# Two groups of tiles change places in SBUF: the split sums of a seven-product scheme and the raw weight blocks it works on

## The chip, the core and the metric

The kernel runs on one core of a Trainium2 chip. The metric is the device time of one execution in microseconds (us). TensorE (PE) multiplies, VectorE (DVE) and ScalarE (ACT) do elementwise work, GpSimd (POOL) does a few small operations, and SyncE (SP) issues most of the DMA transfers. SBUF is the on-chip memory: 128 partitions, each a row of bytes. A tile has the same byte range in every partition.

## The reference, cut to what matters

Two decoder layers over 256 tokens of width 1024. Each layer is a half-step SwiGLU FFN, a token mixer, and a second half-step FFN, with a layer norm behind each.

```python
def swiglu(x, wg, wu, wd):
    return (jax.nn.silu(x @ wg) * (x @ wu)) @ wd
...
    for l in range(DEPTH):
        x = layer_norm(ALPHA * x + 0.5 * swiglu(x, ffn_wg[l, 0], ffn_wu[l, 0], ffn_wd[l, 0]), ln_g[l, 0], ln_b[l, 0])
        m = token_mix(x, w_in[l], w_out[l], cmp_pe[l], cmp_w1[l], cmp_w2[l], pool_w[l], pool_scale[l],
                      gla_wa2[l], gla_ba[l], gla_norm_g[l])
        x = layer_norm(ALPHA * x + m, ln_g[l, 1], ln_b[l, 1])
        x = layer_norm(ALPHA * x + 0.5 * swiglu(x, ffn_wg[l, 1], ffn_wu[l, 1], ffn_wd[l, 1]), ln_g[l, 2], ln_b[l, 2])
```

So there are four FFNs (called FFN 1 to 4 here) and two token mixers, one between FFN 1 and 2, one between FFN 3 and 4. The token mixer compresses keys and values (this uses `cmp_w1`, 1 MB in its expanded form), and computes attention scores.

## The kernel before

**Precision.** Every float32 operand of a large product is split in two parts (`hi` or `wh`: a rounded copy that ACT writes; `lo` or `wl`: the rest, that DVE subtracts). One product is three matmuls: hi by hi, hi by rest, rest by hi. The activations are the stationary operand (128 by 128), the weights the moving one (128 by 512).

**Weights.** A weight block of 512 KB (a tile of 128 by 1024) is loaded by SP into a `raw` tile (four of them rotate), split by ACT (L229) and DVE (L230) into `wh` and `wl` (eight of each rotate), and used by PE. Units of two blocks are made one to three units ahead of PE.

**The pairs.** In the middle part of each FFN six of the eleven gate/up chunks are done in three pairs S4, S6, S8 with seven products for eight: `seven` loads the raw blocks `fa` (b11), `fb` (b12), `fc` (b22) and a `raw` (b21) and subtracts them from one another in place; `make_sums` builds, once for each FFN, four split sums of the quarters of the activation stream, `sa0`, `sa1` and the two halves of `sb`. Products 1, 2 and 4 of a pair use quarters of the stream as they are (`xh`, `xl`), products 5, 6, 7 and 3 use the split sums. Each product is 12 matmuls of line L415. The order of all this is written out by hand and kept:

```python
PLAN = ("a2 T0 b2 S4 1 a3 5 b3 6 T2 d0 7 d1 3 4 2 S6 d2 1 5 T4 d3 6 a10 7 b10 3 4 2 "
        "S8 1 d4 5 T6 6 d5 T10 7 d6 3 4 2 d7 T8").split()
```

A number is a product, `d` a down projection (L262 to L264 on `hi`, `lo`), `T` the transposes of two finished chunks (L490) and their split into `hi` and `lo` (L267, L268), `a` and `b` ordinary gate/up chunks. After the plan come the down projections d10, d8, d9, a layer norm and the next stage.

**Places.** Tiles with the same tag of a pool share one place, and a new tile waits until the last use of the one before it there. A pool's tiles lie one behind another in the order in which the tags first occur. Tags that matter here:

| tag (pool) | bytes of a partition | tiles that take turns in it before |
|---|---|---|
| `ksh`, `ksl` (`cst`) | 25120, 29216 (4096 each) | `sa0`, `sa1`; the mixer's split keys (read by all attention scores) |
| `s_w1` (`cst`) | 16928 (8192) | `sb`; the mixer's compression weight `s_w1` |
| `qs0`, `qs1` (`mix`) | 180992, 185088 (4096 each) | `fa` (two blocks); the mixer's queries |
| `fb0`, `fb1` (`wp`) | 121600, 125696 (4096 each) | `fb` alone (two blocks) |

The pool `cst` also holds small constants; one of them, `mhalf`, takes 32 bytes, and so all tiles of `cst` behind it start 32 bytes past a multiple of 128. The tiles of `wp`, `act` (`xh`, `xl`) and of `mix` up to `pT` start at multiples of 128.

**The compression weight.** The mixer's small tensors are loaded by `layer_small` (L535). For layer 0 it is called at S8 of FFN 1 and its transfers go through SP's queue; for layer 1 they go through POOL's queue. The tile `s_w1` can be loaded when the tile ahead of it in its place has been read for the last time: `sb` is last read by product 3 of S8. `compress` reads `s_w1` in L665, in the mixer.

Of the kernel before, what the change touches and what calls it, by code (L numbers as in the profile page):

```python
# [18 lines left out]
F32 = mybir.dt.float32  # L19
F32R = mybir.dt.float32r  # L20
# [37 lines left out]
def build(ctx, tc, d):  # L58
# [3 lines left out]
    cst = ctx.enter_context(tc.tile_pool(name="cst", bufs=1))  # L62
    wp = ctx.enter_context(tc.tile_pool(name="wp", bufs=1))
    act = ctx.enter_context(tc.tile_pool(name="act", bufs=1))
    mix = ctx.enter_context(tc.tile_pool(name="mix", bufs=2))
# [52 lines left out]
    for t in range(2):  # L118
        vbd.append(cst.tile([128, 2, 2, 64], F32, name=f"vbd{t}"))
        a = cst.tile([128, 4, 128], F32, name=f"at{t}")  # L120
# [11 lines left out]
    def gate_up(l, f, c, q):  # L132
        return [d["wgu"][l, f, c, 2 * q + h] for h in range(2)]

    def seven(l, f, c):


        b11, b12, b21, b22 = [], [], [], []

        def load(to, src, pool, name, tags, bufs):  # L140
            for a, tag in zip(src, tags):
                to.append(pool.tile([128, 1024], F32, name=name, tag=tag, bufs=bufs))
                last_dma[0] = nc.sync.dma_start(out=to[-1], in_=a)

        def less(a, b, to):
            for x, y, z in zip(a, b, to):
                DVE.tensor_sub(out=z, in0=x, in1=y)  # L147

        def parts(ts):
            return [split_tile(x, 1024) for x in ts]  # L150

        def f1():
            load(b11, gate_up(l, f, c, 0), mix, "fa", ("qs0", "qs1"), 1)
            return parts(b11)

        def f5():
            load(b12, gate_up(l, f, c + 1, 0), wp, "fb", ("fb0", "fb1"), 1)
            less(b12, b11, b11)
            return parts(b11)

        def f6():
            load(b22, gate_up(l, f, c + 1, 1), mix, "fc", ("pT", "pT"), 3)
            less(b22, b11, b11)
            return parts(b11)

        def f7():
            less(b22, b12, b12)
            return parts(b12)

        def f4():  # L170
            load(b21, gate_up(l, f, c, 1), wp, "raw", ("raw", "raw"), 4)
            less(b21, b11, b11)
            return parts(b11)

        return {"1": f1, "5": f5, "6": f6, "7": f7, "3": lambda: parts(b22), "4": f4, "2": lambda: parts(b21)}

    for l in range(L):
# [37 lines left out]
    def split_tile(raw, w):  # L215
        wh, wl = split_tiles()
        ACT.activation(out=wh[:, :w], in_=raw[:, :w], func=AF.Copy)  # L217
        DVE.tensor_sub(out=wl[:, :w], in0=raw[:, :w], in1=wh[:, :w].bitcast(F32))  # L218
        return wh, wl
# [46 lines left out]
    def split(hi, lo, src):  # L266
        ACT.activation(out=hi, in_=src, func=AF.Copy)  # L267
        DVE.tensor_sub(out=lo, in0=src, in1=hi.bitcast(F32))  # L268
# [41 lines left out]
    def make_sums(sums):  # L310

        s1, a11, a12, a21 = sums["s"], sums[0, 0], sums[0, 1], sums[1, 0]
        big = cst.tile([128, 2, 2, 4, 128], F32R, name="sb", tag="s_w1")

        def parts(f, i):
            tl = cst.tile([128, 2, 4, 128], F32R, name=f"sa{i}", tag=("ksh", "ksl")[i]) if i < 2 else big[:, i - 2]
            split(tl[:, 0], tl[:, 1], f.rearrange("p (a b) -> p a b", a=4))
            return tl[:, 0], tl[:, 1]
        first = parts(s1, 0)
        DVE.tensor_sub(out=s1, in0=s1, in1=a11)  # L320
        DVE.tensor_sub(out=a21, in0=a11, in1=a21)
        DVE.tensor_sub(out=a12, in0=a12, in1=s1)
        yield first
        yield parts(s1, 1)
        yield parts(a21, 2)
        yield parts(a12, 3)
# [39 lines left out]
    class Ffn:  # L366
# [51 lines left out]
        def plan(self):  # L418
            a = [[tuple(p[:, 4 * q:4 * q + 4] for p in XT[t]) for q in range(2)] for t in range(2)]
            left = {"1": a[0][0], "2": a[0][1], "4": a[1][1]}  # L420
            sums = make_sums(self.sums)

            def f32():
# [691 lines left out]
```

## Time and profile before

| | |
|---|---|
| median of 3 runs | 977.65 us (976.71 to 978.5) |
| profiled execution, its own time | 978.65 us |
| its span, first to last instruction | 976.9 us |
| mean granted TensorE clock | 0.998 |
| PE busy | 960.0 us (98% of the span), 4611 matmuls |
| DVE busy | 843.0 us (86%) |
| ACT busy | 583.8 us (60%) |
| DMA moved | 178.80 MB, mean 183 GB/s |

The profile shows one execution. A matmul's record overlaps the next one's, so the pace of PE is read from the starts of its matmuls, or from the chain that ended last, where a piece lasts until the next begins. "Idle before" is the time in which an engine ran nothing, with what ended it. Times in a row are from the span's start.

### The profile page before, as it was taken

The numbers are of one execution on the slowest core, as the hardware profiler recorded it, in microseconds if no ns is written. First come the engines' busy times: TensorE is split into PE (matmuls) and PEld (weight loads), VectorE is DVE, ScalarE is ACT, GpSimd is POOL, SyncE is SP. The second block draws the span as 40 slices with busy tenths as digits, with TensorE's granted clock in tenths as the row PEclk, the third lists the DMA queues.
The fourth block names the chain that finished last, engine by engine and source line by source line (L and its number), as shares of the span: only waits on it lengthen the run. The fifth ranks groups of instructions, "written<-read, shape, count | busy, mean of one in ns | idle before, by whom it ended". The sixth has DMA issues, their size and how long they took to land.

```text
span 976.9 us, 12852 instructions
## 1 busy us (share of the span) xinstructions
PE 960.0 (98%) x4611; PEld 780.8 (80%) x4611; DVE 843.0 (86%) x1247; ACT 583.8 (60%) x884; POOL 34.7 (4%) x50
## 2 busy tenths in 40 slices
PE   8999999999999999999999999999999999999996
PEld 5888888778778888888788888878787788888885
DVE  6988997988869997999899799978887599899995
ACT  6666665566654666666565666655676366666660
POOL 0000000020001000000000000001000010000000
PEclk9999999999999999999999999999999999999999
DMA  8865666564444645638673746465534374647241
GB/s 282 320 200 169 208 213 237 185 193 144 139 163 141 210 156 189 206 138 280 200 241 119 241 129 225 138 247 186 178 109 137 123 222 148 212 151 237 93 167 43
DMA packets 51872, 178.80 MB, mean 183 GB/s; under 512 B 6624, under 2 KB 7648, under 8 KB 51552
## 3 DMA queue, kind: packets, MB, share of 16 engines
q1 hardware_dynamic: 49968, 171.23, 52.6%
q0 software_dynamic: 1840, 6.75, 2.3%
q8 instruction: 36, 0.59, 0.2%
q14 instruction: 28, 0.23, 0.1%
HBM read 176.91 MB, written 1.05 MB: 182 GB/s over the span
## 4 chain that ended last, share of the span: by engine, by line
PE 86%; DVE 6%; DMA 4%; ACT 2%; issue 2%; SPq 0%; DVEq 0%; ACTq 0%
PE g L415 12%; PE acc L264 11%; PE acc L262 11%; PE acc L263 11%; PE tr L415 8%; PE g L262 4%; PE g L263 4%; PE g L264 4%; PE tr L264 3%; PE tr L263 3%; PE tr L262 3%; DMA raw<-in_wd 3%; PE tr L290 3%; PE acc L281 2%; DVE wl L230 2%
## 5 line engine op out<-in xcount | busy, mean ns | idle before, releaser
L230 DVE TENSOR_TENSOR wl<-raw,wh 128x1024 fp32r<-128x1024 f32 (+2 forms) x225 | 266.7, 1201 | 42.3 <-ACT wh L229 40.9
L229 ACT ACTIVATE wh<-raw 128x1024 fp32r<-128x1024 f32 (+2 forms) x225 | 231.3, 1039 | 113.4 <-PE acc L264 55.4
L217 ACT ACTIVATE wh<-fa 128x1024 fp32r<-128x1024 f32 x96 | 101.7, 1060 | 87.3 <-DVE fa L147 44.3
L264 PE MATMUL acc<-wh,lo 128*128 128x512 f32 x352 | 137.7, 391 | 2.0 <-DVE lo L268 2.0
L262 PE MATMUL acc<-wh,hi 128*128 128x512 f32 x352 | 138.6, 394 | 0.0
L263 PE MATMUL acc<-wl,hi 128*128 128x512 f32 x352 | 137.1, 390 | 0.0
L218 DVE TENSOR_TENSOR wl<-fa,wh 128x1024 fp32r<-128x1024 f32 x96 | 116.4, 1220 | 17.9 <-ACT wh L217 16.3
L263 PE MATMUL g<-wl,xh 128*128 128x512 f32 (+1 forms) x224 | 85.6, 382 | 1.3 <-DVE wl L230 1.3
L264 PE MATMUL g<-wh,xl 128*128 128x512 f32 (+1 forms) x224 | 85.6, 382 | 0.0
L262 PE MATMUL g<-wh,xh 128*128 128x512 f32 (+1 forms) x224 | 85.2, 381 | 0.0
L264 PEld LDWEIGHTS acc<-wh,lo 128*128 128x128 f32 x352 | 66.1, 188 | 17.2 <-DVE lo L268 3.3
L262 PEld LDWEIGHTS acc<-wh,hi 128*128 128x128 f32 x352 | 66.1, 188 | 13.8 <-ACT hi L267 0.5
L263 PEld LDWEIGHTS acc<-wl,hi 128*128 128x128 f32 x352 | 66.1, 188 | 13.4
L263 PE MATMUL acc<-wl,xh 128*128 128x512 f32 x128 | 51.4, 402 | 1.0 <-DVE wl L230 1.0
L262 PE MATMUL acc<-wh,xh 128*128 128x512 f32 x128 | 51.0, 400 | 0.5 <-ACT wh L229 0.5
L264 PE MATMUL acc<-wh,xl 128*128 128x512 f32 x128 | 50.8, 397 | 0.0
L262 PE MATMUL tr<-wh,xh 128*128 128x512 f32 x128 | 50.2, 392 | 0.0
L264 PE MATMUL tr<-wh,xl 128*128 128x512 f32 x128 | 49.9, 390 | 0.0
L263 PE MATMUL tr<-wl,xh 128*128 128x512 f32 x128 | 49.8, 389 | 0.0
L263 PEld LDWEIGHTS g<-wl,xh 128*128 128x128 f32 x224 | 42.1, 188 | 9.5 <-DVE wl L230 2.1
L262 PEld LDWEIGHTS g<-wh,xh 128*128 128x128 f32 x224 | 42.2, 188 | 8.1 <-issue 0.8
L264 PEld LDWEIGHTS g<-wh,xl 128*128 128x128 f32 x224 | 42.1, 188 | 7.1
(287 smaller groups left out, 1937.1 us busy)
## 6 DMA issues: line engine op xcount, KB each, us to landing
raw<-in_wgu SPq DMA_DIRECT2D x103, 512.0 KB, 4.2
raw<-in_wd SPq DMA_DIRECT2D x88, 512.0 KB, 4.5
raw<-in_win SPq DMA_DIRECT2D x32, 512.0 KB, 4.3
fa<-in_wgu SPq DMA_DIRECT2D x24, 512.0 KB, 4.1
fb<-in_wgu SPq DMA_DIRECT2D x24, 512.0 KB, 4.5
fc<-in_wgu SPq DMA_DIRECT2D x24, 512.0 KB, 4.7
raw<-in_wout SPq DMA_DIRECT2D x16, 512.0 KB, 3.9
lnp_ln_g<-in_ln_g POOLq DMA_DIRECT2D x5, 512.0 KB, 5.2
```

The source lines that it names most:

```text
L217: ACT.activation(out=wh[:, :w], in_=raw[:, :w], func=AF.Copy)
L218: DVE.tensor_sub(out=wl[:, :w], in0=raw[:, :w], in1=wh[:, :w].bitcast(F32))
L229: ACT.activation(out=wh[:, s], in_=raw[:, s], func=AF.Copy)
L230: DVE.tensor_sub(out=wl[:, s], in0=raw[:, s], in1=wh[:, s].bitcast(F32))
L262: pe(PE.matmul(ps, xh, wh, start=start, stop=False))
L263: pe(PE.matmul(ps, xh, wl, start=False, stop=False))
L264: pe(PE.matmul(ps, xl, wh, start=False, stop=stop))
L281: PE.matmul(out, lhsT, rhs, start=False, stop=True, skip_group_check=True)
L290: last_pe[0] = PE.transpose(p[:, i * 128:(i + 1) * 128], s, ident)
L415: pe(PE.matmul(ps, a[:, k, :], w[:, s], start=first and k == 0 and n == 0, stop=k == 3 and n == 2, skip_group_check=True))
```

## The change

The sums go where the raw blocks were, and the raw blocks where the sums were: `sa0`, `sa1` take `qs0`, `qs1` of the pool `mix`; `sb` takes a place of 8192 bytes in `wp` (tag `fb`); `fa` takes `ksh`, `ksl`; and `fb`, now one tile of two blocks, takes `s_w1`. No engine instruction and no transfer is added or removed; sizes are the same.

```diff
         def load(to, src, pool, name, tags, bufs):
-            for a, tag in zip(src, tags):
-                to.append(pool.tile([128, 1024], F32, name=name, tag=tag, bufs=bufs))
+            whole = cst.tile([128, 2, 1024], F32, name=name, tag=tags) if pool is cst and len(tags[0]) == 1 else None
+            for i, (a, tag) in enumerate(zip(src, tags)):
+                to.append(whole[:, i] if whole is not None else pool.tile([128, 1024], F32, name=name, tag=tag, bufs=bufs))
                 last_dma[0] = nc.sync.dma_start(out=to[-1], in_=a)
...
         def f1():
-            load(b11, gate_up(l, f, c, 0), mix, "fa", ("qs0", "qs1"), 1)
+            load(b11, gate_up(l, f, c, 0), cst, "fa", ("ksh", "ksl"), 1)
             return parts(b11)
 
         def f5():
-            load(b12, gate_up(l, f, c + 1, 0), wp, "fb", ("fb0", "fb1"), 1)
+            load(b12, gate_up(l, f, c + 1, 0), cst, "fb", "s_w1", 1)
             less(b12, b11, b11)
             return parts(b11)
...
-        big = cst.tile([128, 2, 2, 4, 128], F32R, name="sb", tag="s_w1")
+        big = wp.tile([128, 2, 2, 4, 128], F32R, name="sb", tag="fb", bufs=1)
 
         def parts(f, i):
-            tl = cst.tile([128, 2, 4, 128], F32R, name=f"sa{i}", tag=("ksh", "ksl")[i]) if i < 2 else big[:, i - 2]
+            tl = (mix.tile([128, 2, 4, 128], F32R, name=f"sa{i}", tag=("qs0", "qs1")[i], bufs=1) if i < 2
+                  else big[:, i - 2])
             split(tl[:, 0], tl[:, 1], f.rearrange("p (a b) -> p a b", a=4))
```

## Rows read from the trace of the kernel before

**Rows 1.** The page, part 1: busy us, share of the span, instructions.
```profile
PE 960.0 (98%) x4611; PEld 780.8 (80%) x4611; DVE 843.0 (86%) x1247; ACT 583.8 (60%) x884; POOL 34.7 (4%) x50
```
**Rows 2.** Waits of PE: who, for whom; us in total, times, longest.
```profile
PE acc L264 <- DVE lo L268: 2.0, 3, 0.8
```
**Rows 3.** Timeline of PE, ends of FFN 1, 2, 3: start, us, what, idle before.
```profile
176.54 0.50 PE L264 MATMUL acc<-wh,lo 128*128 128x512 f32 x1 [0.65 <-DVE lo L268]
...
475.91 0.50 PE L264 MATMUL acc<-wh,lo 128*128 128x512 f32 x1 [0.50 <-DVE lo L268]
...
657.17 0.51 PE L264 MATMUL acc<-wh,lo 128*128 128x512 f32 x1 [0.84 <-DVE lo L268]
```
**Rows 4.** Chain that ended last, 120 to 180 us: start, us, what.
```profile
121.05 8.24 PE tr L415 x36
129.29 2.72 PE g L415 x12
...
137.46 2.79 PE g L415 x12
...
150.06 0.76 DVE lo L268 x2
...
158.73 4.62 DMA raw<-in_wd
...
165.80 7.66 DMA raw<-in_wd
...
175.80 0.69 DVE lo L268
```
**Rows 5.** Instructions of L415: ns min/median/max, first and last start, forms.
```profile
L415 PE MATMUL g<-wh,sa x128: 392/395/478, 53.2 to 923.6; 128*128 128x512 f32 x128
...
L415 PE MATMUL g<-wh,sb x128: 392/395/476, 70.6 to 940.6; 128*128 128x512 f32 x128
...
L415 PE MATMUL g<-wh,xh x96: 389/389/393, 45.0 to 945.5; 128*128 128x512 f32 x96
```
**Rows 6.** Instructions on the tiles hi: columns as in rows 5.
```profile
L262 PE MATMUL acc<-wh,hi x352: 387/389/501, 65.0 to 968.2; 128*128 128x512 f32 x176
```
**Rows 7.** Timeline of SP: start, us, DMA issues.
```profile
144.10 1.43 SPq L143 DMA_DIRECT2D fb<-in_wgu  x2
...
160.89 0.33 SPq L535 DMA_DIRECT2D s_w<-in_w  x1
161.31 4.82 SPq L226 DMA_DIRECT2D raw<-in_wd  x4
```
**Rows 8.** Chain that ended last, whole span: ends of FFN 2 and 3.
```profile
467.63 5.20 DMA raw<-in_wgu
...
645.99 6.73 DMA raw<-in_wd
```
**Rows 9.** Waits of POOL: columns as in rows 2.
```profile
POOL s_w L535 <- PE g L415: 141.2, 1, 141.2
```
**Rows 10.** Timeline of DVE, 142 to 146 us.
```profile
142.82 2.35 DVE L218 TENSOR_TENSOR wl<-fb,wh 128x1024 fp32r<-128x1024 f32 x2
```
**Rows 11.** Instructions on the tile s_w, 220 to 240 us: columns as in rows 5.
```profile
L665 PE MATMUL tr<-zB,s_w x16: 275/275/275, 228.4 to 230.1; 128*128 128x60 f32 x16
```
**Rows 12.** Timeline of SP, mixer of layer 0.
```profile
235.96 2.63 SPq L226 DMA_DIRECT2D raw<-in_wout  x2
...
274.88 0.33 SPq L143 DMA_DIRECT2D fa<-in_wgu  x1
```
**Rows 13.** Timeline of ACT, mixer of layer 0.
```profile
245.40 1.05 ACT L229 ACTIVATE wh<-raw 128x1024 fp32r<-128x1024 f32 x1
```
**Rows 14.** Instructions on the tiles fa, 300 to 360 us: columns as in rows 5.
```profile
L217 ACT ACTIVATE wh<-fa x6: 1042/1062/1067, 328.9 to 348.0; 128x1024 fp32r<-128x1024 f32 x6
```
**Rows 15.** Groups of DVE by form: busy us, mean ns, idle before.
```profile
L268 DVE TENSOR_TENSOR lo<-tr,hi 128x512 fp32r<-128x512 f32 x24 | 15.4, 683 | 1.2 <-ACT hi L267 0.8
```
**Rows 16.** Instructions on the tile sb: columns as in rows 5.
```profile
L268 DVE TENSOR_TENSOR sb<-a,sb x8: 682/682/684, 19.0 to 831.7; 128x512 fp32r<-128x512 f32 x8
```

## The prediction

> **What bounds the kernel now.** I read the page first. PE is busy for 960.0 of 976.9 us and DVE for 843.0 [rows 1], so the span is a stream of matmuls with very few holes, and a change that adds and removes no instruction can act in two ways only: it closes or opens holes in that stream, or it alters the pace of the stream itself. So I went on to PE's waits and to the chain.
>
> The waits: the largest entry is 2.0 us in three waits, each of a matmul for a `lo` that DVE had not yet split [rows 2]. They lie at the same place of three FFNs, in the down projections that need the transposes T8: 0.65 us at the end of FFN 1, 0.50 in FFN 2, 0.84 in FFN 3 [rows 3]. That is the whole prize on the side of the holes that touches the tiles of this change; the other holes of PE lie at the start, in the last layer norm and in the mixers' gates, and none of them is a wait for one of these tiles.
>
> The pace: in the chain each product of a pair stands as one piece of 12 matmuls, and the pieces are not equally long. In S8 of FFN 1, products 3, 4 and 2 of S6 run together in 8.24 us; product 1 takes 2.72 us, product 5 takes 2.79 us [rows 4]. Product 1 has a quarter of the stream as its stationary operand, product 5 a split sum; 8.24 is once 2.79 and twice 2.72, and of 3, 4 and 2 only product 3 reads a sum. The instructions of L415 say the same: a matmul on `sa` or `sb` has a median of 395 ns, one on `xh` 389 [rows 5]. `hi`, which is also a freshly split tile, has 389 [rows 6]. So it is not splitting that makes them slow. What sets `sa` and `sb` apart from `xh` and `hi` is their place: they alone start 32 bytes past a multiple of 128. After the change they start at a multiple of 128, among the tiles that run at 2.72.
>
> **The change part by part.**
>
> *The sums' place.* Four products of each pair read sums, so 4 by 3 pairs by 4 FFNs is 48 products of 2.79 us. If each falls to 2.72: 48 by 0.07 = 3.36 us. By the records, 576 matmuls by 6 ns is 3.46 us. As PE has no other hole inside the plan, what a product saves moves everything behind it. The exception is the end of FFN 2: there the chain leaves PE at the split of T10 (the like of 150.06 us in FFN 1) and runs through DVE and DMA until `lo` [rows 4, 8], so what products 7 and 3 save behind that point, 2 by 0.07, only lengthens the hole. DVE, busy 86%, may hold back a little more. I take 3.3 us less 0.3 lost there: 3.0 us. Bounds: 0, if the place is not the cause, to 3.5.
>
> [...]
>
> *The compression weight's load, layer 0.* Its 1 MB is issued at 160.89 us, when product 3 of S8 has read `sb` for the last time, right before four `raw` blocks of the down projections [rows 7]. The chain runs through the last of these blocks: 7.66 us from issue to landing, then ACT, DVE, and `lo` at 175.80 behind them on DVE [rows 4]. At the same point of FFN 2, where no such load runs, the block takes 5.20 us [rows 8]. After the change `s_w1` waits for the last read of `fb` in S8 instead, a DVE split that ends at 142.82 + 2.35 = 145.17 us [rows 10]. There stands now, at 144.10, the early load of FFN 2's `fb`, also 1 MB [rows 7]; this one must wait until `compress` has read `s_w1`. So the two loads change places in the queue, the raw blocks behind 145 us see the same bytes as now, and those behind 161 us land 7.66 - 5.20 = about 2.5 us sooner. The hole is 0.65 us [rows 3], so it closes.
>
> *The same in layer 1.* POOL holds the load back for 141.2 us, until the last read of `sb` [rows 9]; the chain's block then takes 6.73 us [rows 8], 1.5 more than 5.20, against a hole of 0.84 us [rows 3]. It closes too. Nothing that PE needs is queued behind POOL's wait before the layer norm. For both: 0.65 + 0.84 = 1.5 us. Bounds: 0.5, if only their excess over the 0.50 of FFN 2 goes (0.15 + 0.34), to 1.5.
>
> *What loses its place.* FFN 2's `fb` can be loaded once `compress` has read `s_w1`, at 230 us [rows 11]; six microseconds before SP issues the first `wout` block at 235.96 [rows 12], which is split only at 245.40 [rows 13], so a load of 1 MB fits in ahead of it. Both blocks of `fa` now wait for the keys, read until the last score of the mixer; the second block of `fa` waits until then already, at 274.88 us [rows 12]. FFN 2 first splits `fa` at 328.9 us [rows 14], 54 us later. Cost 0; if that cover were gone, a 0.5 MB block costs its landing, some 5 us.
>
> *`fb` as one tile.* The next pair's first block waits for the split of both blocks instead of one, half of 2.35 us [rows 10] later; it is needed many products later. Cost 0.
>
> *The elementwise work on moved tiles.* DVE takes 683 ns for a split into `lo` at a multiple of 128 [rows 15] and 682 ns for the same into `sb` [rows 16]. So the place does not matter to DVE, and `fa` and `fb` lose nothing by it; DVE has 14% to spare in any case.
>
> The sum: 3.0 + 1.5 = 4.5 us. The profiled execution took 978.65 us, so it would take 974.15. It stands 1.0 us above the median of the three runs; from the median, 977.65 - 4.5 = **973.2 us**.
>
> **The rivals.**
>
> *Only the pace.* The order that is worked out at compile time is new, and DVE may meet T8 as late as now, or FFN 2's hole may grow as PE gets there sooner. Then about 3.0 us are left: 974.7. For it speaks that FFN 2 has its hole without any load of `s_w1`.
>
> [...]
>
> *Nothing moves*: both fail, 977.6.
>
> *Slower.* SP's queue is in order, so a load of `fb` that is put ahead of the `wout` blocks, and waits for `compress`, holds them back. Now the first is issued at 235.96 and split at 245.40 [rows 12, 13]; with 5.20 us to land [rows 8], up to 4.2 us of delay cost nothing. To end 2 us slower than now in spite of a gain of 4.5 us, each of the two mixers would have to lose 3.3 us, so SP would have to be held for 7.5 us beyond 235.96, to 243.5, and the release that it waits for is at 230 [rows 11]. Where it happens: 979.6 or more.
>
> **How the numbers follow.** Some 0.2%, 2 us, is what a measurement of this kernel can tell from no change, so faster means under 975.7. Both terms: 0.62 (973.2, its own range 972.0 to 974.5). Only the pace: 0.16. Only the holes: 0.10. Nothing: 0.05. Slower: 0.07. Faster: the first two, less a little of the second that falls short: 0.77. No change: 0.16. Slower: 0.07. The range reaches from a full 3.5 + 1.5 us, 972.65, less 0.85 for the scatter of the three runs (977.65 down to 976.71), 971.8, to the holes alone, 976.3.
>
> **What would show it.** In the profile after: products on sums at 2.72 us in the chain and 389 ns in L415's records; if they stay at 2.79 and 395 the place was not the cause. `s_w1` issued near 145 us, in layer 1 some 16 us sooner than now as well, and no load of it among the blocks that follow product 3; the waits of L264 for `lo` down to that of FFN 2. `fb` for FFN 2 issued soon after 230 us with no wait of ACT for a `raw` block behind it. The prediction is wrong if PE gets a new hole in a mixer, or at the head of FFN 2 or 4, or if DVE cannot follow PE's quicker pace and the hole before `lo` grows by what the products save.

## The result, and the profile after

The changed kernel takes 972.84 us (median of 6 runs, 971.81 to 974.46), the kernel before in the same rounds 978.08 us (976.71 to 979.54). The ratio is 0.9946, 95% interval 0.9935 to 0.9957: 5.3 us faster, between 4.2 and 6.4. The forecast was 973.2 us. In the profiled executions the span falls from 976.9 to 971.0 us, by 5.9. The ratios in this document are of fast runs alone; one execution of *swap only* (3406 us) and one of *sa/fa only* (1607 us) are left out by that.

The diff adds lines, so L415 of the kernel before is L417 here, L268 is L269, L264 is L265, L535 is L537; the experiments shift the lines by up to three more.

The page after, part 1:

```profile
PE 956.5 (99%) x4611; PEld 782.4 (81%) x4611; DVE 841.6 (87%) x1247; ACT 583.4 (60%) x884; POOL 35.8 (4%) x50
```

Of the 5.9 us, 960.0 - 956.5 = 3.5 us are PE's busy time [rows 1]; the rest, 2.4 us, are holes: PE stood idle for 16.9 us of the span before and for 14.5 us after. But busy time is not the pace alone, and an idle stretch is shorter than the delay behind it, since a matmul's record of 389 ns runs on over the start of the next, 227 ns later. The cleaner account goes from the start of each matmul to the start of the next; both traces have the same 4611 in the same order:

| where | us less after |
|---|---|
| ahead of the first product of FFN 1 | -0.9 |
| the products of the pairs | 3.3 |
| other matmuls, a little each, many of them next to a product | 0.6 |
| ends of FFN 1, 2 and 3 | 0.93 + 0.67 + 1.34 = 2.9 |
| mixer of layer 1, two waits | 0.5 - 0.5 = 0 |

The pace. The chain that ended last, after, at the same place as [rows 4]:

```profile
121.28 8.16 PE tr L417 x36
129.44 2.72 PE g L417 x12
...
137.60 2.72 PE g L417 x12
```

Product 5, on a sum, now takes the 2.72 us of product 1, and products 3, 4 and 2 together 8.16 us, three times 2.72. For 48 products, 0.07 us each is 3.4 us, as the table above has it within its rounding. The records of L417 after, against [rows 5]:

```profile
L417 PE MATMUL g<-wh,sa x128: 389/389/476, 54.1 to 917.8; 128*128 128x512 f32 x128
...
L417 PE MATMUL g<-wh,sb x128: 389/389/478, 71.3 to 934.7; 128*128 128x512 f32 x128
...
L417 PE MATMUL g<-wh,xh x96: 389/389/389, 45.9 to 939.6; 128*128 128x512 f32 x96
```

The medians of 395 ns are gone; the sums run as the quarters do.

The holes. All of PE's waits after:

```profile
PE tr L291 <- ACT c L641: 1.3, 2, 0.9
PE acc L107 <- DVE zw L110: 1.2, 1, 1.2
PE acc L264 <- DVE wl L231: 1.0, 1, 1.0
PE g L264 <- DVE wl L231: 0.8, 2, 0.6
PE acc L291 <- DMA x<-in_x: 0.8, 1, 0.8
PE tr L667 <- PE acc L282: 0.7, 2, 0.4
PE acc L263 <- ACT wh L230: 0.5, 1, 0.5
```

The wait for `lo` that led the list in [rows 2] is no longer in it: the holes at the ends of FFN 1, 2 and 3 (0.65 + 0.50 + 0.84 = 2.0 us, [rows 3]) have all closed. The transfers that were to close two of them, in SP's timeline and POOL's waits:

```profile
145.52 0.33 SPq L537 DMA_DIRECT2D s_w<-in_w  x1
...
229.31 0.80 SPq L144 DMA_DIRECT2D fb<-in_wgu  x2
234.87 21.26 SPq L227 DMA_DIRECT2D raw<-in_wout  x8
```

```profile
POOL s_w L537 <- DVE wl L219: 124.6, 1, 124.6
```

The compression weight is issued at 145.52 us instead of 160.89 [rows 7], and POOL waits 124.6 us for DVE's split of `fb` where it waited 141.2 for product 3 [rows 9]. FFN 2's `fb` goes out at 229.31, when `compress` lets go of the place, 5.6 us ahead of the `wout` blocks. The raw blocks that are issued between 157 and 167 us now land in 5.0 us; the four behind the compression weight took 8.7 us before:

```profile
raw<-in_wd SPq DMA_DIRECT2D x6, 512.0 KB, 5.0
```

### The profile page after: what moved, and what is told of

Same layout as the page of the kernel before. It is cut to its first block, busy times and chain, and to the rows that moved or that the text cites. A ratio compares the mean times of both kernels' runs of the same rounds, so it can differ in the third digit from the quotient of the medians.

```text
span 971.0 us, 12847 instructions
## 1 busy us (share of the span) xinstructions
PE 956.5 (99%) x4611; PEld 782.4 (81%) x4611; DVE 841.6 (87%) x1247; ACT 583.4 (60%) x884; POOL 35.8 (4%) x50
## 4 chain that ended last, share of the span: by engine, by line
PE 94%; DVE 3%; issue 1%; ACT 1%; DMA 0%; SPq 0%; DVEq 0%
PE g L417 16%; PE acc L263 12%; PE acc L264 12%; PE acc L265 12%; PE tr L417 8%; PE g L263 4%; PE g L264 4%; PE g L265 4%; PE tr L264 3%; PE tr L265 3%; PE tr L263 3%; PE tr L291 3%; PE acc L282 2%; PE tr L492 1%; PE tr L282 1%
## 5 line engine op out<-in xcount | busy, mean ns | idle before, releaser
L265 PE MATMUL acc<-wh,lo 128*128 128x512 f32 x352 | 137.3, 390 | 0.0
L264 PE MATMUL acc<-wl,hi 128*128 128x512 f32 x352 | 137.0, 389 | 0.0
L264 PE MATMUL g<-wl,xh 128*128 128x512 f32 (+1 forms) x224 | 85.6, 382 | 0.8 <-DVE wl L231 0.8
L265 PE MATMUL g<-wh,xl 128*128 128x512 f32 (+1 forms) x224 | 85.5, 382 | 0.0
L265 PEld LDWEIGHTS acc<-wh,lo 128*128 128x128 f32 x352 | 66.1, 188 | 14.2 <-DVE lo L269 0.3
L264 PEld LDWEIGHTS acc<-wl,hi 128*128 128x128 f32 x352 | 66.1, 188 | 13.4
L264 PE MATMUL acc<-wl,xh 128*128 128x512 f32 x128 | 51.6, 403 | 1.0 <-DVE wl L231 1.0
L265 PE MATMUL acc<-wh,xl 128*128 128x512 f32 x128 | 51.1, 399 | 0.0
L265 PE MATMUL tr<-wh,xl 128*128 128x512 f32 x128 | 49.8, 389 | 0.0
L264 PE MATMUL tr<-wl,xh 128*128 128x512 f32 x128 | 49.8, 389 | 0.0
L264 PEld LDWEIGHTS g<-wl,xh 128*128 128x128 f32 x224 | 42.1, 188 | 9.0 <-DVE wl L231 1.7
L265 PEld LDWEIGHTS g<-wh,xl 128*128 128x128 f32 x224 | 42.1, 188 | 7.0
```

Source lines behind the costliest of these rows:

```text
L264: pe(PE.matmul(ps, xh, wl, start=False, stop=False))
L265: pe(PE.matmul(ps, xl, wh, start=False, stop=stop))
```

## The experiments

Twelve runs. Five were timed against the kernel before in five rounds; each of the others is one profiled execution.

**One part each: the start of the sums, and the exchange without it.** In *start only* every tile of the kernel before keeps its tag and its neighbours, but padding shifts the sums, and the other tiles of `cst` behind `mhalf`, by 96 bytes, so that the sums start at a multiple of 128.

```diff
-    mhalf = cst.tile([128, 4], F32, name="mhalf")
+    mhalf = cst.tile([128, 32], F32, name="mhalf")     # 96 bytes more ahead of the sums
...
-        ld("wa2", [128, 128], d["wa2"][l])
+        ld("wa2", [128, 136], d["wa2"][l])             # 32 bytes more behind them; 128 columns used
```

> The kernel before with every tile in its old place, but with the pool cst padded by 96 bytes ahead of the sums and 32 behind, so that the sums start at a multiple of 128 bytes. Theory (the start of the sums sets the pace): products 5, 6, 7, 3 at 2.72 us and 389 ns as in the changed kernel; the three holes before lo (0.65, 0.50, 0.84 us) stay within 0.3 us each; time about 3.0 to 3.5 us under the kernel before, ratio 0.9965 to 0.997. Rival (the pool or the neighbours of a tile set it, not its start): products stay at 2.79 us and 395 ns, ratio 0.999 to 1.001.

In *swap only* the exchange is made, and the sums are moved on by 32 bytes in their new places.

```diff
-        big = wp.tile([128, 2, 2, 4, 128], F32R, name="sb", tag="fb", bufs=1)
+        big = wp.tile([128, 2112], F32R, name="sb", tag="fb", bufs=1)
...
+            off = (8, 8, 8, 8)[i]
+            tl = (mix.tile([128, 1056], F32R, name=f"sa{i}", tag=("qs0", "qs1")[i], bufs=1) if i < 2
+                  else big[:, (i - 2) * 1056:(i - 1) * 1056])
+            tl = tl[:, off:off + 1024].rearrange("p (s a b) -> p s a b", s=2, a=4)
```

> The changed kernel with the sums moved on by 32 bytes inside their new places. Theory (start and order of loads are two separate gains): products on sums back at 2.79 us and 395 ns, PE busy 3.5 us longer than in the changed kernel, the holes of FFN 1 and 3 gone, since the compression weight still loads early; ratio to the kernel before 0.9975 to 0.998. FFN 2's hole tells why it closed in the changed kernel: if it is back at 0.5 us, the quicker pace closed it; if it stays closed, the new order of loads did. Rival (the place in SBUF as such): products stay at 2.72 us and the ratio at 0.9946.

| run | ratio to before, 95% interval | span | PE busy |
|---|---|---|---|
| start only | 0.9976 (0.9961 to 0.9991) | 972.2 | 955.7 |
| swap only | 0.9984 (0.9973 to 0.9995) | 974.6 | 959.8 |

Start only, records of its L416, and its waits of PE:

```profile
L416 PE MATMUL g<-wh,sa x128: 389/389/476, 53.1 to 919.0; 128*128 128x512 f32 x128
...
L416 PE MATMUL g<-wh,sb x128: 389/389/481, 70.3 to 935.9; 128*128 128x512 f32 x128
```

```profile
PE acc L265 <- DVE lo L269: 1.2, 2, 0.8
```

The padding alone brings the sums to 389 ns in their old tags, pool and neighbours, and PE's busy time down by 4.3 us. So tag, pool and neighbours are not what makes the sums slow. Two of the three waits for `lo` remain, 0.36 us in FFN 2 and 0.84 us in FFN 3. That of FFN 1, which I expected to stay, is gone in this execution, though the compression weight is still issued just ahead of four raw blocks, at 159.81 us. Start only, DMA issues from 159 us on (us to landing last):

```profile
raw<-in_wd SPq DMA_DIRECT2D x4, 512.0 KB, 6.7
s_w<-in_w SPq DMA_DIRECT2D x1, 1024.0 KB, 4.8
```

Both landed sooner than in the kernel before (8.7 and 7.6 us, shown below). So in FFN 1 a late megabyte does not open the hole in every execution. Swap only, its chain (products 1, 5 and 6), and its waits of PE:

```profile
44.67 2.72 PE g L419 x12
52.84 2.79 PE g L419 x12
61.09 2.80 PE g L419 x12
```

```profile
PE acc L265 <- DVE lo L269: 0.3, 1, 0.3
```

32 bytes take the pace back, and the holes of FFN 1 and 3 stay closed (the 0.3 us is FFN 2's). The two gains are separate. By the ratios (2.3 and 1.6 us) they add to less than the 5.3 of the whole, but each interval is 1.1 to 1.5 us wide to either side.

**One half of the exchange each.** *sa/fa only* keeps `sb` and `fb` as before, *sb/fb only* keeps `sa0`, `sa1` and `fa`.

```diff
 sa/fa only, against the changed kernel
-            load(b12, gate_up(l, f, c + 1, 0), cst, "fb", "s_w1", 1)
+            load(b12, gate_up(l, f, c + 1, 0), wp, "fb", ("fb0", "fb1"), 1)
...
-        big = wp.tile([128, 2, 2, 4, 128], F32R, name="sb", tag="fb", bufs=1)
+        big = cst.tile([128, 2, 2, 4, 128], F32R, name="sb", tag="s_w1")
 sb/fb only, against the changed kernel
-            load(b11, gate_up(l, f, c, 0), cst, "fa", ("ksh", "ksl"), 1)
+            load(b11, gate_up(l, f, c, 0), mix, "fa", ("qs0", "qs1"), 1)
...
-            tl = (mix.tile([128, 2, 4, 128], F32R, name=f"sa{i}", tag=("qs0", "qs1")[i], bufs=1) if i < 2
-                  else big[:, i - 2])
+            tl = cst.tile([128, 2, 4, 128], F32R, name=f"sa{i}", tag=("ksh", "ksl")[i]) if i < 2 else big[:, i - 2]
```

> One half of the change: sa0, sa1 and fa exchange places, sb and fb stay as before. Theory: products 5 and 6 (24 of 48) at 2.72 us, 7 and 3 at 2.79, so 1.7 us less of PE; the compression weight still waits for sb and is issued near 160 us and, in layer 1, near 640 us, so the holes of FFN 1 and 3 stay at 0.5 to 0.9 us; ratio 0.998 to 0.9985. Rival (the holes close because of the quicker pace or the new place of fa, not because the weight loads early): the holes are gone, ratio 0.9955 to 0.9965.

> The other half: sb and fb exchange places, sa0, sa1 and fa stay as before. Theory: products 7 and 3 at 2.72 us, 5 and 6 at 2.79, 1.7 us less of PE; the compression weight is issued near 145 us and near 623 us, the holes of FFN 1 and 3 are gone; ratio 0.9960 to 0.9968. Rival as in the other half: the holes stay, ratio 0.998 to 0.9985. FFN 2's hole shows whether fb as one tile, whose second block now loads later, is what closed it: gone here and present in the other half if so.

sa/fa only: 0.9982 (0.9972 to 0.9991), sb/fb only: 0.9963 (0.9950 to 0.9976), both ratios as the theory had them; 1.8 + 3.6 = 5.4 us, about the whole. The waits of PE and then of POOL, first in sa/fa only, then in sb/fb only:

```profile
PE acc L265 <- DVE lo L269: 1.6, 3, 0.8
```

```profile
POOL s_w L537 <- PE g L417: 140.7, 1, 140.7
```

```profile
PE acc L265 <- DVE lo L269: 0.6, 1, 0.6
```

```profile
POOL s_w L536 <- DVE wl L219: 125.0, 1, 125.0
```

Where `sb` still blocks the compression weight, all three holes are there (0.44, 0.28 and 0.84 us); where it does not, those of FFN 1 and 3 are gone, and the one left is FFN 2's, 0.64 us. So `fb` as one tile did not close that one.

**The load of the compression weight by itself.** In the kernel before, one sixteenth of the weight is loaded.

```diff
+            if nm == "w1":
+                q.dma_start(out=tl[:, 0:1], in_=src[:, 0:1])
...
-                PE.matmul(hp[:, 0:60], sm["w1"][:, ab * 8 + pp, :], ...
+                PE.matmul(hp[:, 0:60], sm["w1"][:, 0, :], ...
```

> The kernel before, with one sixteenth of the compression weight loaded and used sixteen times over (fifteen sixteenths of that weight are left out of the computation); its transfer still waits for sb at the same place of the queue. Theory (the megabyte of the load delays the raw blocks and opens the holes of FFN 1 and 3): the blocks behind 161 us land in 5 to 6 us, both holes are gone, products on sums stay at 2.79 us, the span is about 1.5 us shorter than before. Rival (the waiting for sb at the head of the queue opens the holes): they stay at 0.6 to 0.9 us.

DMA issues from 160.5 us on, for the kernel before and then for this one (us to landing last):

```profile
raw<-in_wd SPq DMA_DIRECT2D x4, 512.0 KB, 8.7
s_w<-in_w SPq DMA_DIRECT2D x1, 1024.0 KB, 7.6
```

```profile
raw<-in_wd SPq DMA_DIRECT2D x5, 512.0 KB, 5.4
s_w<-in_w SPq DMA_DIRECT2D x1, 64.0 KB, 3.4
```

With the wait at the same place and only the bytes gone, the raw blocks land in 5.4 us instead of 8.7; of the holes, 0.14 us is left in FFN 1 and none in FFN 2 and 3. The span is 975.9 us, 1.0 less than the 976.9 of the kernel before. So the megabyte opened the holes, not the wait. In FFN 3 that is plain: 0.84 us stands in each of the four profiles with a late megabyte (the kernel before twice, start only, sa/fa only) and nothing without it. In FFN 1 the same four have 0.65, 0.55, 0 and 0.44 us; there it depends on how fast the blocks land, 8.7, 8.5, 6.7 and 8.3 us.

**How far one execution differs from the next.** Both kernels once more.

> The kernel before once more, on this chip, to see how far the holes and landings of one profiled execution differ from the next. If they are set by the kernel: holes of 0.65, 0.50 and 0.84 us within 0.1, the block in the chain of FFN 1 at 7.7 us within 0.3. If one execution is chance: they differ by 0.3 us and more.

> The changed kernel once more. If FFN 2's hole is closed by the kernel's order: no hole at the end of FFN 2, as in its first profile. If it is chance: a hole of 0.3 to 0.6 us, as the run with the sums moved on by 32 bytes (0.31) and the one with the exchange of sb and fb alone (0.64) had.

Kernel before again, and changed kernel again, timeline of PE at the end of FFN 2:

```profile
476.25 0.50 PE L264 MATMUL acc<-wh,lo 128*128 128x512 f32 x1 [0.19 <-DVE lo L268]
```

```profile
473.04 0.39 PE L264 MATMUL acc<-wl,hi 128*128 128x512 f32 x1
473.53 0.50 PE L265 MATMUL acc<-wh,lo 128*128 128x512 f32 x1
```

FFN 1 and 3 repeat: 0.55 and 0.84 us before, none after. FFN 2 does not: 0.50 and 0.19 before, none and 0.10 (473.43 to 473.53) after. Over all runs it lies between 0 and 0.64 with no order that I can see; two kernels with the changed kernel's pace and order of loads have 0.42 (*Can it be carried further?*) and 0.27 (*all by 32*). So its closing in the changed kernel's first profile was most likely chance, worth up to 0.5 of the 5.9 us of span. The spans here are 978.7 and 971.2 us. PE's busy time is 961.6 before, 1.6 more than in the first profile (mean granted clock 0.994 against 0.998), and 956.5 after, so a difference of busy times between two executions can be off by as much; the pieces of the chain are 2.79 and 2.72 us again.

**Which offsets cost.** As swap only, but with the four sums moved on by different amounts.

```diff
-            off = (8, 8, 8, 8)[i]
+            off = (4, 16, 24, 12)[i]      # first run: 16, 64, 96, 48 bytes
+            off = (20, 28, 2, 16)[i]      # second run: 80, 112, 8, 64 bytes
```

> The changed kernel with the four sums moved on by 16 bytes (sa0, product 5), 64 (sa1, product 6), 96 (first half of sb, product 7) and 48 (second half, product 3). Theory with a granule of 64 bytes: products 5, 7 and 3 take 2.79 us, product 6 takes 2.72. With a granule of 128: all four take 2.79. [...]

> As the run with four offsets, with 80 bytes (sa0, product 5), 112 (sa1, product 6), 8 (first half of sb, product 7) and 64 (second half, product 3). That run gave 2.72 us at 16, 2.75 at 64, 2.80 at 96 and 2.77 at 48. Theory A (the offset inside 128 bytes alone counts): 64 gives 2.75 again, though in another tile and product; 112 and 80 lie between 2.72 and 2.80; 8 gives more than 2.72. Theory B (the tile or product counts, not the offset): product 3 gives 2.77 again, product 6 gives 2.75.

The chain of the first run, then of the second; the pieces are products 5, 6 and 7 of S4 and then 3, 4 and 2 together:

```profile
53.12 2.72 PE g L419 x12
61.28 2.75 PE g L419 x12
70.38 2.81 PE g L419 x12
78.64 8.21 PE g L419 x36
```

```profile
52.63 2.78 PE g L419 x12
60.88 2.72 PE g L419 x12
69.95 2.77 PE g L419 x12
78.16 8.19 PE g L419 x36
```

| bytes moved on | 0 | 8 | 16 | 32 | 48 | 64 | 80 | 96 | 112 |
|---|---|---|---|---|---|---|---|---|---|
| us for a product | 2.72 | 2.77 | 2.72 | 2.79 | 2.76 | 2.75 | 2.78 | 2.81 | 2.72 |

(48 is from the starts of product 3's matmuls, 78.47 us, to the first of product 4, 81.23; the second 64 is 8.19 less twice 2.72.) The second run's 64, in another tile and product, gives 2.75 again. No granule of 64 or 128 bytes explains the row: 16 and 112 take the 2.72 us of 0, and 64 takes 2.75.

**Start or distance?** Until here the weights, the moving operand, always started at a multiple of 128. Two kernels move them as well: *all by 32* shifts the weights and the large products' stationary operands alike, *weights by 32* the weights alone (the sums' tile there is moved by 96 bytes more, to a multiple of 128).

```diff
 all by 32, against the changed kernel (the pools behind cst shift)
-        ld("wa2", [128, 128], d["wa2"][l])
+        ld("wa2", [128, 136], d["wa2"][l])             # 32 bytes more; 128 columns used
 weights by 32, against the changed kernel
+    pad0 = wp.tile([128, 8], F32, name="pad0")         # 32 bytes ahead of raw, wh, wl
...
-        big = wp.tile([128, 2, 2, 4, 128], F32R, name="sb", tag="fb", bufs=1)
+        big = wp.tile([128, 2072], F32R, name="sb", tag="fb", bufs=1)[:, 24:2072]
```

> The changed kernel with every tile of the pools wp, act and mix moved on by 32 bytes, the weights (moving operands) and all stationary operands alike. Theory (the stationary operand's own start counts): the some 3700 matmuls of the large products all take 5.5 ns more, 395 ns in the records and 2.79 us a product, time about 20 us over the changed kernel, near 993. Rival (what counts is the distance between stationary and moving operand modulo 128): products at 2.72 us and the time near 973.

> The changed kernel with raw, wh and wl, the moving operands, moved on by 32 bytes, the sums and all stationary operands at multiples of 128. Theory (the stationary operand's own start counts): products at 2.72 us, time near 973. Rival (the distance counts): all products at 2.79 us or more, time near 993. If the start matters to transfers too, raw blocks land later than the 4.1 to 4.6 us of the changed kernel, and holes open where PE is fed just in time.

All by 32 (span 970.1 us), instructions on its tiles `hi`; weights by 32 (span 992.0), the same, then its chain:

```profile
L263 PE MATMUL acc<-wh,hi x352: 387/389/478, 64.8 to 961.5; 128*128 128x512 f32 x176
```

```profile
L265 PE MATMUL acc<-wh,hi x352: 392/397/479, 66.3 to 983.3; 128*128 128x512 f32 x176
```

```profile
46.03 2.81 PE g L420 x12
54.47 2.81 PE g L420 x12
```

My theory of the start falls. With everything 32 bytes past a multiple of 128 nothing is slow: no product in its chain takes 2.79. With the weights alone moved, every product is slow, at 2.80 or 2.81 us in its chain, those on untouched quarters too, and PE is busy for 977.4 us instead of 956.5. The transfers did not mind: the raw blocks land in 4.4 us (median) against 4.3. And 2.81 is the price that a sum moved on by 96 bytes had: weights 32 ahead and stationary operand 96 ahead are the same distance modulo 128. What sets the pace is the distance between the starts of the two operands. That it counts modulo 128 fits swap only, too: there one sum lies 4224 bytes, 33 times 128, behind the other in `mix`, and products 5 and 6 take 2.79 and 2.80 us.

**Can it be carried further?** The changed kernel with the pool `cst` padded as in start only, so that the mixer's tiles in it stand at multiples of 128 too.

> The changed kernel with the pool cst padded by 96 bytes ahead of the big tiles and 32 behind, so that fa, fb, the compression weight, the keys and the mixer's constants start at multiples of 128 bytes too. Theory (only a stationary operand's start matters, and few are left in cst): 0 to 0.6 us under the changed kernel, ratio to the kernel before 0.9940 to 0.9948. Rival (the start matters to transfers and elementwise work as well): fa and fb land sooner than 4.5 and 5.7 us and DVE's and ACT's splits of them are shorter, ratio under 0.993.

0.9945 (0.9931 to 0.9959), not to be told from the changed kernel's 0.9946. The rival fails: ACT's and DVE's splits of `fa` have medians of 1062 and 1221 ns, 1062 and 1218 in the changed kernel. No run here beats the changed kernel clearly.

## Why the prediction was right, step by step

*The bound.* Right: PE's stream has few holes, and the gain is the sum of its pace and of holes closed at the ends of FFNs.

*The sums' place.* The size was right, forecast 3.36 to 3.46 us by the rows and 3.0 after a deduction, measured 3.3 in the products themselves and 0.6 in other matmuls, many of them their neighbours, which I had not counted. The deduction of 0.3 is not borne out: FFN 2's hole did not grow, but it scatters by more than that. The reason that I gave was half right. "They alone start 32 bytes past a multiple of 128" was true, and moving them was what helped, but the runs put the distance to the weights in the place of the start. In the kernel before the two readings are one, as every weight started at a multiple of 128; only moving the weights told them apart.

*The compression weight.* Right in both layers: issued 15 us sooner in layer 0 and 19 in layer 1 (641.67 to 622.34 us), the two holes closed, 1.5 us of idle time in the first profiles and 0.55 + 0.84 = 1.4 in the second. I took that idle time for the gain; from start to start the two holes had cost 0.93 + 1.34 = 2.3 us, so this term was too small. The halves, and the load of one sixteenth, show that it is its megabyte ahead of the raw blocks that made them late. What I did not see is that FFN 1's hole depends on how fast these blocks land in an execution: with the same order of loads it was 0 in start only.

*FFN 2's hole.* I let it stay. It closed in one profile and was 0.10 us in the next; it scatters from run to run, before the change as well. With that, and with the two terms above, the profiled span fell by more than forecast, although the start was 0.9 us slower after. The timed gain is 5.3 us, and its interval, 4.2 to 6.4, holds the forecast 4.5. That the time lies only 0.4 us from the forecast is in part luck: the gain was 0.8 us more than forecast, and the kernel before took 0.4 us more than the 977.65 that the forecast started from.

*What loses its place.* Right: `fb` at 229.31 us lies ahead of the `wout` blocks, and ACT has no wait for a raw block there. In the mixers some waits moved (one for a transpose of layer 1 grew from 0.41 to 0.93 us, one for a split shrank from 0.65 to 0.19), for nothing in sum.

*The rivals.* Only the pace, and only the holes, both exist as kernels now (start only, swap only), and each gives a part of the gain. The latter, to which I gave 0.10, would have left the sums at 2.79 us for another reason than their place; that fails, as they take 2.72 after the change, and 32 bytes alone bring the 2.79 back (swap only). Slower had no trace. One sum of the range is off: the three runs scatter by 977.65 - 976.71 = 0.94 us and not 0.85; nothing hangs on it.

## What to carry to other kernels

When two groups of otherwise equal instructions differ by two or three per cent in a profile, as 2.79 and 2.72 us do here, look for what differs in their operands' addresses, and look at all operands of the instruction: here a tile of 32 bytes, declared far away, cost some 3.4 us. And a place that two tiles share ties their times together: look which load a long-lived tile holds back, and what stands in the queue behind it when it is let go: here `sb` held the compression weight back until 160.89 us [rows 7], just ahead of four raw blocks that took 8.7 us to land, and `fb` until 145.52, after which the raw blocks of 157 to 167 us landed in 5.0.

## What the runs showed of the hardware

A float32r matmul of 128 by 128 by 512 takes 2.72 us for twelve when its stationary and moving operand start at the same place modulo 128 bytes, and up to 2.81 us (3% more) at other distances, by the distance as in the table above; 16 and 112 bytes take 2.72 like 0. Each of these figures is one product of one execution; the median over the twelve pairs of its run lies within 0.01 us of it. On all large products at once this is worth 992.0 - 971.0 = 21 us of this kernel (weights by 32 against the changed kernel). What in the chip makes it so, no run shows, nor whether what counts is the stationary operand that a matmul uses or the one that is loaded beside it (188 ns for each, in PEld's records). The elementwise engines did not mind: DVE's split into `sb` took 682 ns at an offset of 32 [rows 16] and 684 in the changed kernel, ACT's 616 and 613.
